# Convolution edges to VectorE, its tap and rest a step later; modulation group 5 into pass two; the second quarter's roots earlier

## The chip, the cores and the metric

The kernel runs on 1 core of a Trainium2 chip. The metric is the device time of one execution in microseconds (us), the median of several runs. One core has five engines with queues of their own: TensorE (PE: matrix products and transposes into PSUM), VectorE (DVE), ScalarE (ACT), GpSimd (POOL) and SyncE (SP, which here only issues transfers). Each engine works its queue strictly in the program's order; an instruction that waits holds up all that stand behind it on its engine. Transfers (DMA) are issued from the queues of SP and POOL and run beside the engines.

## The reference

One layer of a diffusion backbone over 2048 tokens of 1024 channels, with a short gated convolution as the mixer and an expert-choice mixture of 16 experts:

```
m = silu(c) @ ada_w + ada_b;  sh1, sc1, g1, sh2, sc2, g2 = split(m, 6)
h  = rms_norm(x, norm_g[0]) * (1 + sc1) + sh1
gate_b, gate_c, v = split(h @ w_in, 3)
x1 = x + g1 * ((gate_b * dwconv3(gate_c * v, conv_w)) @ w_out)
h2 = rms_norm(x1, norm_g[1]) * (1 + sc2) + sh2
aff = softmax(h2 @ router);  each expert takes its 256 best tokens
out = x1 + g2 * scatter_add(gate * (silu(xs @ wg) * (xs @ wu)) @ wd)
```

`dwconv3` is a depthwise convolution over 3 neighbouring tokens: y[t] = w0 u[t-1] + w1 u[t] + w2 u[t+1]. All is float32; each matrix product is made of three products of parts (high x high, low x high, high x low).

## The kernel before

The scheduling is by hand: on each engine the instructions stand in the order in which the Python code calls them.

*The input product* h @ w_in takes the 2048 tokens as four quarters of 512. First come two channel blocks of the first quarter and the second (`in_mm`, `in_out`), while the modulation's columns and the normalized rows come in. The loop over `g` in 0..3 does the first quarter; in its last round the second quarter's four blocks of 128 rows are prepared: a sum of squares (`rstd_of`, line 287 on ScalarE or 285 on VectorE), a root in two GpSimd operations (288, 290), and a scaling of the rows (`norm_x`, 415 or 417). `to_hl` then transposes them on TensorE (424).

*The two passes.* What is left of the product runs in 148 steps. A *unit* is two blocks of products for two halves; it has seven steps of 12 matmuls (lines 869 to 871), the seven products of a fast 2x2 block scheme, summed into three PSUM banks. Steps 0 to 63 are pass one (quarters one and two), where unit 8 has eight steps without the scheme (56 to 63); steps 64 to 147 are pass two (quarters three and four). Units come in threes: two make `gate_c` and `v` of a channel block, the third the `gate_b` of both. `unit_step` issues a step's products and copies a bank out on ScalarE (933) after steps 0, 1, 2, 4 and 6 of a unit; step 2 adds onto the bank of step 0, so its first product waits for the copy-out of step 0. VectorE adds a bank to the copied rows one step later (935). The blocks of weights are made three or four steps ahead: a high part on ScalarE (848), a low part on VectorE (849), and sums of blocks on VectorE (855 to 861).

*The order around the change.* `at(n, f)` puts a function into step n's list; the list runs before the step's own products. Behind the last step n of a unit of the first kind, `conv_start` is put at n + 1 (the product gate_c * v on VectorE, 881; the edge columns `v[:, 0:2]` from `carry` by a GpSimd copy, 882, in pass two a cleared last column, 884; the middle tap on ScalarE, 886) and `conv_rest` at n + 2 (the outer taps on VectorE, 890 and 892, and in pass one the edge kept in `carry`, 895). Behind a unit of the second kind `conv_gate` is put at n + 1 and n + 2 (900; a store to `vscr` from GpSimd's queue, 903 or 905, and a kept column, 906). The rows of a unit lie in five buffers, `wide`.

*Modulation groups 2 to 5* (g1, sh2, sc2, g2) are each a sum over eight blocks of 128 rows of `ada_w`. `ada_step(g, t)` adds block t - 1 on VectorE (562, 564), loads block t + 1 from GpSimd's queue (551) into one of four buffers `b4`, and at t = 9 ends the group: two products with a matrix of ones on TensorE (571) and two additions (572); groups 2 to 4 are then stored to `rows` (576). Group 5 stands at steps 36 to 47, groups 3, 2, 4 at steps 68 to 136, one t every 11/4 steps. The same buffers `b4` hold the rows `fu` that `load_full` and `refill` bring for pass two from step 47 to 67.

*Constants* for the later search are made by a generator, one piece at each of steps 4 to 43; `group_of` fills two tiles on GpSimd (120, 128) and compares them on VectorE (121 to 130).

Of the kernel before, what the change touches and what calls it, by code (L numbers as in the profile page):

```python
# [7 lines left out]
F32 = mybir.dt.float32  # L8
# [9 lines left out]
P = 128  # L18
# [28 lines left out]
def block_kernel(ctx: ExitStack, tc, x, c, ada_w, ada_b, norm_g, w_in, conv, w_out, router, wg, wu, wd, out):  # L47
# [63 lines left out]
    def constants(scratch):  # L111
        before = consts.tile([P, P], BF, name="before")
        nc.vector.tensor_scalar(before, jp, 0.0, None, op0=ALU.is_gt)
        ones_b = consts.tile([P, 1], BF, name="ones_b")
        nc.vector.memset(ones_b, 1.0)

        def group_of(name, shift, mask, pattern):

            row = consts.tile([P, 1], I32, name=name + "_i")
            nc.gpsimd.iota(row, pattern=[[0, 1]], base=0, channel_multiplier=1)  # L120
            nc.vector.tensor_scalar(row, row, shift, mask, op0=ALU.logical_shift_right, op1=ALU.bitwise_and)
            rowf = consts.tile([P, 1], F32, name=name + "_r")
            nc.vector.tensor_copy(rowf, row)
            n = 1
            for _, m in pattern:
                n *= m
            col = scratch("col", n)
            nc.gpsimd.iota(col, pattern=pattern, base=0, channel_multiplier=0, allow_small_or_imprecise_dtypes=True)
            t = consts.tile([P, n], F32R, name=name)
            nc.vector.tensor_scalar(t, col, rowf, None, op0=ALU.is_equal)  # L130
            return t, rowf

        yield
        same, _ = group_of("same", 3, E - 1, [[1, E], [0, 8]])
        yield
        sameq, _ = group_of("sameq", 3, NF - 1, [[0, P // (8 * NF)], [1, NF], [0, 8]])
        yield
        rep, repf = group_of("rep", 5, 3, [[1, 4]])
        block, _ = group_of("block", 5, 3, [[1, 4], [0, 32]])
        yield  # L140
        tri = consts.tile([P, P], BF, name="tri")
        nc.vector.tensor_mul(tri, block.bitcast(F32), before)
        mult = consts.tile([P, 5], F32, name="mult")
        nc.gpsimd.iota(mult, pattern=[[4, 5]], base=1, channel_multiplier=0, allow_small_or_imprecise_dtypes=True)
        nc.vector.tensor_scalar(mult, mult, repf, None, op0=ALU.add)
        stepq = consts.tile([P, N_FEW[0] + N_FEW[1], 3], F32, name="stepq")
        biasq = consts.tile([P, N_FEW[0] + N_FEW[1], 2], F32, name="biasq")
        for i in range(N_FEW[0] + N_FEW[1]):
            lo = i >= N_FEW[0]
            unit = 1.0 if lo else float(1 << LOW_FEW)  # L150
            if i % 3 == 0:
                yield
            st = unit * float(FEW) ** (N_FEW[0] + lo * N_FEW[1] - 1 - i)
            nc.gpsimd.tensor_scalar(stepq[:, i], mult[:, 0:3], st, None, op0=ALU.mult)
            nc.gpsimd.tensor_scalar(biasq[:, i], mult[:, 3:5], -st, 0.5 * unit, op0=ALU.mult, op1=ALU.add)
        yield
        needq = consts.tile([P, 5, 4], F32, name="needq")
        nc.gpsimd.memset(needq[:, 0:3], float(CAP))
        nc.gpsimd.memset(needq[:, 3:5], float(2 * CAP - L))
        slot_r = consts.tile([P, P], BF, name="slot_r")  # L160
        nc.gpsimd.iota(slot_r, pattern=[[1, P]], base=0, channel_multiplier=0,
                       allow_small_or_imprecise_dtypes=True)
        yield
        step = consts.tile([P, N_HI + N_LO], F32, name="step")
        bias = consts.tile([P, N_HI + N_LO, 2], F32, name="bias")
        for i in range(N_HI + N_LO):
            if i % 5 == 4:
                yield
            st = (1 << LOW) * 4.0 ** (N_HI - 1 - i) if i < N_HI else 4.0 ** (N_HI + N_LO - 1 - i)
            nc.gpsimd.memset(step[:, i:i + 1], st)  # L170
            for j in range(2):
                nc.gpsimd.memset(bias[:, i, j:j + 1], 0.5 * (float(1 << LOW) if i < N_HI else 1.0) - (j + 2) * st)
        need = consts.tile([P, 3], F32, name="need")
        nc.gpsimd.memset(need[:, 0:1], float(CAP))
        nc.gpsimd.memset(need[:, 1:3], float(2 * CAP - L))
        zero1 = consts.tile([P, 4], F32, name="zero1")
        nc.gpsimd.memset(zero1, 0.0)
        cnts = [consts.tile([P, 4], F32R, name=f"cnt{i}") for i in range(2)]
        zero1 = zero1[:, 0:1]
        aux = consts.tile([P, E, NB, 5], BF, name="aux")  # L180
        yield
        nc.gpsimd.iota(aux[:, :, :, 0], pattern=[[0, E], [0, NB]], base=0, channel_multiplier=1,
                       allow_small_or_imprecise_dtypes=True)
        yield
        nc.gpsimd.iota(aux[:, :, :, 1], pattern=[[0, E], [1, NB]], base=0, channel_multiplier=0,
                       allow_small_or_imprecise_dtypes=True)
        quick = sameq, rep, stepq, biasq, needq
        return before, ones_b, tri, slot_r, step, bias, need, zero1, cnts, aux, same, quick
# [180 lines left out]
    with tc.tile_pool(name="mix", bufs=1) as mix, ExitStack() as ctx_mixd:  # L369
# [63 lines left out]
        def low_x(q, k, full):  # L433
            nc.vector.tensor_sub(hl[q, k][:, 1], full, hl[q, k][:, 0].bitcast(F32))
# [213 lines left out]
        for g in range(4):  # L648
            k = 2 * g
            more_g = g < 3  # L650
            ada_fix(g, 0)
            full = scale_x(0, k)
            ada_fix(g, 1)
            if g:
                low_w(g, 1)
                low_w(g, 2)
            if more_g:
                ada_cols(g + 1, 0, 1)
            low_x(0, k, full)
            keep(k, full)  # L660
            mm_pair(0, k)
            turn_x(0, k + 1)
            full = scale_x(0, k + 1)
            if more_g:
                ada_cols(g + 1, 1, 5)
            low_x(0, k + 1, full)
            keep(k + 1, full)
            mm_pair(1, k)
            if more_g:
                turn_x(0, k + 2)  # L670
                high_w(g + 1)
                ada_cols(g + 1, 5, KD)
            else:
                rs = [rstd_of(xq[1][b], junk_tile()) for b in range(4)]
                for b in range(4):
                    norm_x(1, b, None, rs[b])
            mm_pair(0, k + 1)
            if g < 2:
                load_ada_cols(g + 2)
                load_w(g + 2)  # L680
            if g == 1:
                load_x(1)
            if more_g:
                ada_sum(g + 1)
                low_w(g + 1, 0)
            else:
                in_out(pair[0], 0, 0)
                to_hl(1, 0)
            mm_pair(1, k + 1)
# [188 lines left out]
        def conv_start(ps_, ct, c, v):  # L878

            o = v[:, 2:2 + 2 * QT]  # L880
            nc.vector.tensor_mul(o, c[:, 2:2 + 2 * QT], o)
            nc.gpsimd.tensor_copy(v[:, 0:2], carry[:, ct, 0:2])
            if ps_:
                nc.gpsimd.memset(v[:, 2 * QT + 2:2 * QT + 3], 0.0)
            n = 2 * QT + ps_
            nc.scalar.activation(c[:, 0:n], v[:, 1:1 + n], AF.Copy, scale=cw[1][:, ct:ct + 1])

        def conv_rest(ps_, ct, c, v):
# [3 lines left out]
            nc.vector.scalar_tensor_tensor(c[:, 0:n], v[:, 2:2 + n], cw[2][:, ct:ct + 1], c[:, 0:n],  # L892
                                           op0=ALU.mult, op1=ALU.add)
            if not ps_:
                nc.gpsimd.tensor_copy(carry[:, ct, 0:2], v[:, n:n + 2])

        def conv_gate(ps_, ct, gate):
            n = 2 * QT + ps_
# [2 lines left out]
            if ps_:  # L901
                nc.gpsimd.tensor_mul(c[:, 0:1], c[:, 0:1], carry[:, ct, 2:3])
                nc.gpsimd.dma_start(vscr[:, ct, L - n:L], c[:, 0:n])
            else:
                nc.gpsimd.dma_start(vscr[:, ct, 0:n - 1], c[:, 1:n])
                nc.gpsimd.tensor_copy(carry[:, ct, 2:3], gate[:, n + 1:n + 2])

        def behind_unit(u, n, x, y):
            (m, ct), (_, ct2) = units[u]
# [4 lines left out]
            else:  # L914
                convs[ct] = x
                at(n + 1, lambda: conv_start(ps_, ct, x, y))
                at(n + 2, lambda: conv_rest(ps_, ct, x, y))

        q0, q1 = slice(2, 2 + QT), slice(2 + QT, 2 + 2 * QT)

# [78 lines left out]
        for n in range(4):  # L999
# [9 lines left out]
            at(25 + 4 * n, lambda j=n: save_sums(j))  # L1009
            at(27 + 4 * n, lambda j=n: save_last(j))  # L1010
            at(47, lambda s=n: load_full(6 + s))
        for t in range(KD + 2):
            at(36 + t * 5 // 4, lambda t=t: ada_step(5, t))
        for s, n in enumerate((51, 52, 53, 54, 55, 56, 57, 58, 59, 60, 61, 62, 64, 65, 66, 67)):
            at(n, lambda s=s: refill(6 + s))
        for t in range(3 * KD + 2):
            for i, g in enumerate((3, 2, 4)):
                if 0 <= t - KD * i < KD + 2:
                    at(n1 + 4 + t * 11 // 4, lambda g=g, t=t - KD * i: ada_step(g, t))
        made = []  # L1020
        consts_of = constants(lambda name, n: hl_tile([P, n], F32, name))

# [749 lines left out]
```

## Time and profile before

| | us |
|---|---|
| median of 3 runs | 1869.77 (1867.82 to 1870.92) |
| the profiled execution | 1868.36 |
| its span, first to last instruction | 1866.3 |
| TensorE busy in it | 1798.3 |
| VectorE, ScalarE, GpSimd busy | 1276.3, 916.9, 333.1 |
| mean granted clock of TensorE | 0.986 |

In the profile's rows a line's instructions stand as `out<-in` with the tiles' names; a bracket such as `[2.16 <-ACT cx L933]` is the idle time of the engine just before, and what ended it. The granted clock (PEclk) is 1.00 at full speed and 0.50 at half. The first pass runs from about 105 to 302 us, the second to 543 us; then come the output product and router to about 750 us, the search, and the experts to the end.

### The profile page before, as it was taken

The page shows a single profiled execution, that of the slowest core. Times are in us where ns is not written, and L with a number is a line of the kernel's source. Part 1 is how long each engine was busy: PE and PEld are TensorE (multiplying, and loading weights), DVE is VectorE, ACT ScalarE, POOL GpSimd, SP SyncE. Part 2 cuts the span into 40 slices and gives each one's busy share as a digit, 9 for nine tenths or more (in the row PEclk, how much of TensorE's full clock was granted, in tenths as well). Part 3 has the DMA queues.
Part 4 walks back from the last instruction along what each step waited for, and adds up shares of the span by engine and source line. Part 5 has one row for each costly group of instructions (what it writes and reads, how often), then busy time and mean ns, then how long its engine had stood idle before and what let it go on. Part 6 is the DMA issues. An engine that isn't in the chain of part 4 may idle for free.

```text
span 1866.3 us, 29372 instructions
## 1 busy us (share of the span) xinstructions
PE 1798.3 (96%) x11415; PEld 1595.0 (85%) x11415; DVE 1276.3 (68%) x1804; ACT 916.9 (49%) x1246; POOL 333.1 (18%) x500
## 2 busy tenths in 40 slices
PE   7999989999999999599999999999999999999997
PEld 6778868878788887498899999999999999999996
DVE  6687777867776677787665765666666576666653
ACT  4555445333345555475454554455455454545541
POOL 2325210101112223100102210210211121021002
PEclk9999999999999999799999999999999999999999
DMA  9656656434467897476878788787878878788774
GB/s 340 206 187 206 224 192 221 150 114 147 136 227 236 246 261 225 149 225 204 223 222 260 222 242 244 250 233 227 262 213 244 259 225 237 233 258 235 224 228 80
DMA packets 309771, 406.78 MB, mean 218 GB/s; under 512 B 103284, under 2 KB 174240, under 8 KB 309632
## 3 DMA queue, kind: packets, MB, share of 16 engines
q1 hardware_dynamic: 283632, 312.59, 55.0%
q0 software_dynamic: 26000, 92.33, 16.7%
q8 instruction: 89, 1.46, 0.3%
q14 instruction: 50, 0.41, 0.1%
HBM read 318.34 MB, written 63.98 MB: 205 GB/s over the span
## 4 chain that ended last, share of the span: by engine, by line
PE 82%; DVE 6%; DMA 4%; issue 4%; ACT 3%; POOL 1%; POOLq 0%; SPq 0%; ACTq 0%; DVEq 0%
PE pm L1595 12%; PE pm L1597 12%; PE pm L1599 12%; PE pm L1664 6%; PE pm L1662 6%; PE pm L1663 6%; PE pm L869 5%; PE pm L870 5%; PE pm L871 5%; PE pm L1124 2%; PE pm L1125 2%; PE pm L1127 2%; DMA hl<-hl 1%; PE pm L511 1%; PE pm L512 1%
## 5 line engine op out<-in xcount | busy, mean ns | idle before, releaser
L248 DVE TENSOR_TENSOR ws<-raw,ws 128x1024 fp32r<-128x1024 f32 x390 | 463.5, 1221 | 273.9 <-ACT ws L238 273.5
L238 ACT ACTIVATE ws<-raw 128x1024 fp32r<-128x1024 f32 x390 | 394.3, 1052 | 410.0 <-PE pm L1599 325.6
L1595 PE MATMUL pm<-xT,ws 128*128 128x256 f32 x2048 | 568.6, 278 | 1.3 <-ACT xT L1574 1.3
L1597 PE MATMUL pm<-xT,ws 128*128 128x256 f32 x2048 | 567.3, 277 | 1.9 <-DVE xT L1575 1.8
L1599 PE MATMUL pm<-xT,ws 128*128 128x256 f32 x2048 | 566.8, 277 | 0.0
L1597 PEld LDWEIGHTS pm<-xT,ws 128*128 128x128 f32 x2048 | 386.0, 188 | 3.9 <-DVE xT L1575 2.1
L1595 PEld LDWEIGHTS pm<-xT,ws 128*128 128x128 f32 x2048 | 385.9, 188 | 3.0 <-ACT xT L1574 1.8
L1599 PEld LDWEIGHTS pm<-xT,ws 128*128 128x128 f32 x2048 | 385.9, 188 | 0.0
L1692 POOL DMA_INDIRECT out_dram<-ot,idx x30 | 104.9, 3498 | 588.8 <-DVE ot L1681 584.8
L1664 PE MATMUL pm<-ws,hT 128*128 128x512 f32 x504 | 198.3, 394 | 0.0
L1662 PE MATMUL pm<-ws,hT 128*128 128x512 f32 x504 | 198.1, 393 | 0.0
L1663 PE MATMUL pm<-ws,hT 128*128 128x512 f32 x504 | 197.0, 391 | 0.0
L869 PE MATMUL pm<-tg,sb 128*128 128x512 f32 x472 | 187.2, 397 | 8.2 <-ACT cx L933 8.1
L871 PE MATMUL pm<-tg,sb 128*128 128x512 f32 x472 | 184.6, 391 | 0.0
L870 PE MATMUL pm<-tg,sb 128*128 128x512 f32 x472 | 184.5, 391 | 0.0
L849 DVE TENSOR_TENSOR sb<-raw,sb 128x512 fp32r<-128x512 f32 x144 | 98.5, 688 | 85.8 <-ACT sb L848 85.4
L869 PEld LDWEIGHTS pm<-tg,sb 128*128 128x128 f32 x472 | 89.0, 189 | 31.5 <-ACT cx L933 13.0
L848 ACT ACTIVATE sb<-raw 128x512 fp32r<-128x512 f32 x144 | 88.6, 626 | 53.8 <-DVE raw L855 23.5
L1664 PEld LDWEIGHTS pm<-ws,hT 128*128 128x128 f32 x504 | 94.7, 188 | 20.0
L1663 PEld LDWEIGHTS pm<-ws,hT 128*128 128x128 f32 x504 | 94.6, 188 | 19.8
L1662 PEld LDWEIGHTS pm<-ws,hT 128*128 128x128 f32 x504 | 94.7, 188 | 18.6
L871 PEld LDWEIGHTS pm<-tg,sb 128*128 128x128 f32 x472 | 89.0, 189 | 18.9
(385 smaller groups left out, 2626.4 us busy)
## 6 DMA issues: line engine op xcount, KB each, us to landing
raw<-in_moe_w_down_dram SPq DMA_DIRECT2D x128, 512.0 KB, 4.7
raw<-in_moe_w_gate_dram SPq DMA_DIRECT2D x126, 512.0 KB, 5.1
raw<-in_moe_w_up_dram SPq DMA_DIRECT2D x126, 512.0 KB, 4.1
raw<-in_sc_w_in_dram SPq DMA_DIRECT2D x42, 512.0 KB, 4.4
xt<-in_x_dram SPq DMA_DIRECT2D x32, 512.0 KB, 7.2
aw<-in_ada_w_dram POOLq DMA_DIRECT2D x32, 512.0 KB, 4.1
fu<-fscr SPq DMA_DIRECT2D x23, 512.0 KB, 4.5
hl<-in_ada_w_dram SPq DMA_DIRECT2D x32, 256.0 KB, 6.3
```

The costliest lines, as they stand in the source:

```text
L238: nc.scalar.activation(t[:, 0], raws[n_high], AF.Copy)
L248: (eng or nc.vector).tensor_sub(t[:, 1, ..., s], raw[..., s], t[:, 0, ..., s].bitcast(F32))
L869: nc.tensor.matmul(o, t[:, 0, j], r[:, 0], start=(first and j == 0), stop=False, skip_group_check=True)
L870: nc.tensor.matmul(o, t[:, 1, j], r[:, 0], start=False, stop=False, skip_group_check=True)
L871: nc.tensor.matmul(o, t[:, 0, j], r[:, 1], start=False, stop=end, skip_group_check=True)
L1595: nc.tensor.matmul(o, w[:, 0, j, c0], xT[:, 0, k], start=(k == 0 and f % 2 == 0), stop=False, skip_group_check=True)
L1597: nc.tensor.matmul(o, w[:, 0, j, c0], xT[:, 1, k], start=False, stop=False, skip_group_check=True)
L1599: nc.tensor.matmul(o, w[:, 1, j, c0], xT[:, 0, k], start=False, stop=(k == KD - 1), skip_group_check=True)
L1662: nc.tensor.matmul(ps[s], h, w[:, 0, j], start=(k == 0), stop=False)
L1663: nc.tensor.matmul(ps[s], h, w[:, 1, j], start=False, stop=False)
L1664: nc.tensor.matmul(ps[s], l, w[:, 0, j], start=False, stop=(k == KD - 1))
L1692: st = nc.gpsimd.indirect_dma_start(out=out_rows, out_offset=bass.IndirectOffsetOnAxis(ap=idx_of[e][:, s:s + 1], axis=0), in_=ots[s], in_o ...
```

## The change

Four edits. (1) `group_of` is a generator now: GpSimd's fills come in one step, VectorE's comparisons in the next; two more pauses lie around `block` and `mult`. (2) In the last round of the first quarter the four `rstd_of` of the second quarter move up: blocks 0 and 2 (squares on ScalarE) behind the second `ada_fix`, blocks 1 and 3 (squares on VectorE) behind `low_x`; of the scalings, blocks 0 and 2 go to ScalarE. (3) The convolution's edge copies, cleared columns and kept columns go from GpSimd to VectorE, the edge ahead of the product; the middle tap becomes `conv_tap`, at n + 2, and `conv_rest` goes to n + 3. (4) Group 5 leaves steps 36 to 47 and goes ahead of groups 3, 2, 4 in pass two; the t of all four lie at listed steps 67 to 137: steps 1, 3, 5 of a unit, and 1, 2, 3, 5 of every third unit.

```diff
@@ group_of
             row = consts.tile([P, 1], I32, name=name + "_i")
             nc.gpsimd.iota(row, pattern=[[0, 1]], base=0, channel_multiplier=1)
-            nc.vector.tensor_scalar(row, row, shift, mask, op0=ALU.logical_shift_right, op1=ALU.bitwise_and)
-            rowf = consts.tile([P, 1], F32, name=name + "_r")
-            nc.vector.tensor_copy(rowf, row)
...
             nc.gpsimd.iota(col, pattern=pattern, base=0, channel_multiplier=0, allow_small_or_imprecise_dtypes=True)
+            yield
+            nc.vector.tensor_scalar(row, row, shift, mask, op0=ALU.logical_shift_right, op1=ALU.bitwise_and)
+            rowf = consts.tile([P, 1], F32, name=name + "_r")
+            nc.vector.tensor_copy(rowf, row)
@@ the loop over g
             ada_fix(g, 1)
+            if not more_g:
+                rs = {b: rstd_of(xq[1][b], junk_tile()) for b in (0, 2)}
...
             low_x(0, k, full)
+            if not more_g:
+                rs.update({b: rstd_of(xq[1][b], junk_tile(), nc.vector) for b in (1, 3)})
...
-                rs = [rstd_of(xq[1][b], junk_tile()) for b in range(4)]
                 for b in range(4):
-                    norm_x(1, b, None, rs[b])
+                    norm_x(1, b, None if b % 2 else nc.scalar, rs[b])
@@ conv_start
             o = v[:, 2:2 + 2 * QT]
+            nc.vector.tensor_copy(v[:, 0:2], carry[:, ct, 0:2])
+            if ps_:
+                nc.vector.memset(v[:, 2 * QT + 2:2 * QT + 3], 0.0)
             nc.vector.tensor_mul(o, c[:, 2:2 + 2 * QT], o)
-            nc.gpsimd.tensor_copy(v[:, 0:2], carry[:, ct, 0:2])
-            if ps_:
-                nc.gpsimd.memset(v[:, 2 * QT + 2:2 * QT + 3], 0.0)
+
+        def conv_tap(ps_, ct, c, v):
             n = 2 * QT + ps_
             nc.scalar.activation(c[:, 0:n], v[:, 1:1 + n], AF.Copy, scale=cw[1][:, ct:ct + 1])
@@ conv_rest
-                nc.gpsimd.tensor_copy(carry[:, ct, 0:2], v[:, n:n + 2])
+                nc.vector.tensor_copy(carry[:, ct, 0:2], v[:, n:n + 2])
@@ conv_gate
-                nc.gpsimd.tensor_copy(carry[:, ct, 2:3], gate[:, n + 1:n + 2])
+                nc.vector.tensor_copy(carry[:, ct, 2:3], gate[:, n + 1:n + 2])
@@ behind_unit
                 at(n + 1, lambda: conv_start(ps_, ct, x, y))
-                at(n + 2, lambda: conv_rest(ps_, ct, x, y))
+                at(n + 2, lambda: conv_tap(ps_, ct, x, y))
+                at(n + 3, lambda: conv_rest(ps_, ct, x, y))
@@ the lists of steps
-        for t in range(KD + 2):
-            at(36 + t * 5 // 4, lambda t=t: ada_step(5, t))
...
-        for t in range(3 * KD + 2):
-            for i, g in enumerate((3, 2, 4)):
+        ada_at = [n1 + N_GROUP * v + i for v in range(N_GROUP + 4) for i in ((1, 2, 3, 5) if v and v % 3 == 0 else (1, 3, 5))]
+        ada_at = [n for n in ada_at if n > n1 + 2]
+        for t in range(4 * KD + 2):
+            for i, g in enumerate((5, 3, 2, 4)):
                 if 0 <= t - KD * i < KD + 2:
-                    at(n1 + 4 + t * 11 // 4, lambda g=g, t=t - KD * i: ada_step(g, t))
+                    at(ada_at[t], lambda g=g, t=t - KD * i: ada_step(g, t))
```

More of the change, by code (lines that the diff above doesn't have):

```diff
@@ L133, in constants @@
         yield
-        same, _ = group_of("same", 3, E - 1, [[1, E], [0, 8]])
+        same, _ = yield from group_of("same", 3, E - 1, [[1, E], [0, 8]])
         yield
-        sameq, _ = group_of("sameq", 3, NF - 1, [[0, P // (8 * NF)], [1, NF], [0, 8]])
+        sameq, _ = yield from group_of("sameq", 3, NF - 1, [[0, P // (8 * NF)], [1, NF], [0, 8]])
         yield
-        rep, repf = group_of("rep", 5, 3, [[1, 4]])
-        block, _ = group_of("block", 5, 3, [[1, 4], [0, 32]])
+        rep, repf = yield from group_of("rep", 5, 3, [[1, 4]])
+        yield
+        block, _ = yield from group_of("block", 5, 3, [[1, 4], [0, 32]])
         yield
@@ L144, in constants @@
         nc.gpsimd.iota(mult, pattern=[[4, 5]], base=1, channel_multiplier=0, allow_small_or_imprecise_dtypes=True)
+        yield
         nc.vector.tensor_scalar(mult, mult, repf, None, op0=ALU.add)
```

## The prediction

> **What bounds the kernel now.** I read the page first, then the waits of TensorE, then its busy time in stretches of 20 us, then the timeline around each gap.
>
> ```profile
> PE 1798.3 (96%) x11415; PEld 1595.0 (85%) x11415; DVE 1276.3 (68%) x1804; ACT 916.9 (49%) x1246; POOL 333.1 (18%) x500
> ```
>
> TensorE (PE) is busy 96% of the 1866.3 us span, so only its gaps, and time at a lower clock, can be won. The change touches the program up to the end of pass two, about 540 us. There these stretches are not full (start:end, length, PE busy, then the other engines; PEclk is the granted clock):
>
> ```profile
> 60.00:80.00 20.00, 16.35 (x76) 12.79 (x75) 12.49 (x20) 13.24 (x22) 8.36 (x17) 0.91 0.28 103
> 120.00:140.00 20.00, 17.84 (x79) 14.47 (x78) 14.73 (x31) 10.74 (x20) 8.07 (x20) 1.00 0.34 121
> 200.00:220.00 20.00, 18.98 (x92) 15.53 (x92) 16.14 (x24) 8.97 (x15) 5.71 (x13) 1.00 0.71 239
> 240.00:260.00 20.00, 14.58 (x48) 9.87 (x47) 14.70 (x22) 4.70 (x9) 4.91 (x6) 0.83 0.76 242
> 380.00:400.00 20.00, 17.72 (x69) 13.80 (x68) 12.58 (x17) 6.50 (x12) 1.85 (x5) 0.91 0.44 132
> 460.00:480.00 20.00, 18.78 (x83) 15.19 (x82) 14.37 (x19) 7.49 (x13) 1.45 (x4) 1.00 0.44 127
> ```
>
> Idle PE is 20 minus the first figure: 3.65, 2.16, 1.02, 5.42, 2.28 and 1.22 us. Three stretches also lose clock: 0.91 over 20 us costs 20 x 0.09 = about 1.7 us, 0.83 costs 3.4 us. Who is waited for, in the waits view (total, times, longest; the first row is of the stretch 0 to 80 us):
>
> ```profile
> PE pt L424 <- DVE xt L417: 3.6, 4, 1.1
> PE pm L869 <- ACT cx L933: 8.1, 5, 2.3
> PE pt L571 <- DVE acc L564: 4.0, 1, 4.0
> ```
>
> So three causes: transposes that wait for the second quarter's normalized rows (3.6), block products that wait until ScalarE (ACT) has copied a PSUM bank out (8.1 in five gaps), and the end of modulation group 5 (4.0).
>
> **The change, part by part.** *Convolution.* Why ScalarE is late is seen in the rows around three of the gaps:
>
> ```profile
> 129.03 1.22 DVE L881 TENSOR_TENSOR cy<-cx,cy 128x1024 f32<-128x1024 f32 x1
> 130.36 1.15 ACT L886 ACTIVATE cx<-cy,v_col 128x1024 f32<-128x1024 f32 x1 [3.67 <-DVE cy L881]
> 132.04 0.50 PE L869 MATMUL pm<-tg,sb 128*128 128x512 f32 x1 [2.16 <-ACT cx L933]
> ...
> 242.05 0.60 ACT L933 ACTIVATE cy<-pm 128x512 f32<-128x512 f32 x1 [2.95 <-POOL carry L906]
> ...
> 386.11 0.56 POOL L551 DMA_DIRECT2D aw<-in_ada_w_dram  x1 [2.47 <-DMA rows<-dst]
> 386.67 0.20 POOL L882 COPY cy<-carry 128x2 f32<-128x2 f32 x1
> 386.90 1.15 ACT L886 ACTIVATE cx<-cy,v_col 128x1025 f32<-128x1025 f32 x1 [6.60 <-POOL cy L884]
> ```
>
> The tap L886 stands in ScalarE's queue ahead of the copy L933 of the unit's first product. At 130 us it waits for VectorE (DVE), whose product L881 stands behind constants; at 387 us for a tiny GpSimd (POOL) copy behind a load that itself waits for `rows<-dst`. At 242 us the copy-out itself waits for GpSimd's edge copy L906 to free a buffer. The program's order on ScalarE at the first convolution, before:
>
> ```order
> L848 ACTIVATE sb<-raw 128x512
> L287 ACTIVATE junk,ss<-xt 128x1024
> L886 ACTIVATE cx<-cy,v_col 128x1024
> L933 ACTIVATE cx<-pm 128x512
> L848 ACTIVATE sb<-raw 128x512
> L287 ACTIVATE junk,ss<-xt 128x1024
> L933 ACTIVATE cy<-pm 128x512
> ```
>
> and now (L894 is the tap, L942 the copy-out, L290 the square):
>
> ```order
> L854 ACTIVATE sb<-raw 128x512
> L290 ACTIVATE junk,ss<-xt 128x1024
> L942 ACTIVATE cx<-pm 128x512
> L854 ACTIVATE sb<-raw 128x512
> L290 ACTIVATE junk,ss<-xt 128x1024
> L894 ACTIVATE cx<-cy,v_col 128x1024
> L942 ACTIVATE cy<-pm 128x512
> ```
>
> The tap moved behind the copy of `cx`, which the step after next needs, and now stands ahead of `cy`, which is needed four steps later. On VectorE, at the same place, the product L881 stood before behind two constants (`rep`, `block`) whose first operations wait for GpSimd:
>
> ```order
> L935 TENSOR_TENSOR cx<-cx,pm 128x512
> L849 TENSOR_TENSOR sb<-raw,sb 128x512
> L859 TENSOR_TENSOR raw<-raw 128x512
> L121 TENSOR_SCALAR rep_i<-rep_i 128x1
> L123 CAST rep_r<-rep_i 128x1
> L130 TENSOR_SCALAR rep<-col,rep_r 128x4
> L121 TENSOR_SCALAR block_i<-block_i 128x1
> L123 CAST block_r<-block_i 128x1
> L130 TENSOR_SCALAR block<-col,block_r 128x128
> L881 TENSOR_TENSOR cy<-cx,cy 128x1024
> ```
>
> and now (L890 is the product):
>
> ```order
> L944 TENSOR_TENSOR cx<-cx,pm 128x512
> L855 TENSOR_TENSOR sb<-raw,sb 128x512
> L865 TENSOR_TENSOR raw<-raw 128x512
> L887 COPY cy<-carry 128x2
> L890 TENSOR_TENSOR cy<-cx,cy 128x1024
> L855 TENSOR_TENSOR sb<-raw,sb 128x512
> L867 TENSOR_TENSOR raw<-raw 128x512
> L420 TENSOR_SCALAR xt<-xt,rstd 128x1024
> ```
>
> The constants moved to later steps, and L887, the edge copy taken from GpSimd, stands before the product. Its price:
>
> ```profile
> L882 POOL COPY cy<-carry x14: 178/198/730, 128.1 to 517.3; 128x2 f32<-128x2 f32 x14
> L906 POOL COPY carry<-cy x3: 200/948/2807, 177.7 to 312.7; 128x1 f32<-128x1 f32 x3
> L542 DVE COPY carry<-pm x2: 149/150/150, 98.8 to 111.7; 128x1 f32<-128x1 f32 x2
> ```
>
> 14 + 6 + 6 copies x 0.15 us, and 8 clears of at most that, is 5 us of VectorE spread over 435 us, under products on TensorE; without that cover it is 5 us. The gain is the five gaps: 8.1 us, and the clock at 380 (1.7) with its 2.28 us gap: 9.8. What is late next is the rest (two passes over 1024 columns), a step later; its readers, the gates, come at least a unit (seven steps) later, so I take 0. Bounds: half of the five gaps stay (+4.9), or nothing more.
>
> *Modulation group 5.* In pass one its picks are one step apart:
>
> ```profile
> 249.35 1.29 DVE L564 SCALAR_TENSOR_TENSOR acc<-aw,s_col,acc 128x1024 f32<-128x1024 f32 x1 [1.44 <-DMA aw<-in_ada_w_dram]
> 250.78 3.75 PE L571 MATMUL pt<-acc,ones_f 128*128 128x512 f32 x4 [4.03 <-DVE acc L564]
> ...
> L564 DVE SCALAR_TENSOR_TENSOR acc<-aw,s_col,acc x28: 1276/1279/1286, 226.3 to 505.4; 128x1024 f32<-128x1024 f32 x28
> DMA to landing us min/median/max: 3.9/4.1/7.3
> ```
>
> The last of its eight loads lands late, VectorE waits, TensorE waits 4.03 us and then runs at half clock: 4.03 + 3.4 = 7.4 us leave pass one. Its matmuls L571 only change place. A rule stands against the clock term: the Trainium skill, "TensorE: Matmul & The Clock Gate" (section "What's actually happening"), has the clock halved after an idle window of about 3.4 us. By it the 2.28 us gap at 380 and the 1.14 us pieces at 60 would lose no clock, and the sum would be 3.4 us smaller; the rows have 0.91 in both stretches, so the rows decide.
>
> In pass two eight loads on GpSimd's queue, eight adds of 1.28 and two additions join: 11.6 us of VectorE over some 200. Picks now lie at steps 1, 3, 5 of a unit, and at 2 as well after a gate unit; the gates' stores to `vscr` share GpSimd's queue with the loads. Three of the four ends come two or three steps after the last add. Group 5's comes one step after it. VectorE's order at its end before, in pass one (L564 the last add, L572 the additions behind the matmuls):
>
> ```order
> L564 SCALAR_TENSOR_TENSOR acc<-aw,s_col,acc 128x1024
> L935 TENSOR_TENSOR cx<-cx,pm 128x512
> L849 TENSOR_TENSOR sb<-raw,sb 128x512
> L857 TENSOR_TENSOR raw<-raw 128x512
> L572 TENSOR_TENSOR g2b<-pt,g2b 128x512 x2
> ```
>
> and now, in pass two:
>
> ```order
> L908 TENSOR_TENSOR cx<-cx 128x1024
> L855 TENSOR_TENSOR sb<-raw,sb 128x512
> L567 SCALAR_TENSOR_TENSOR acc<-aw,s_col,acc 128x1024
> L908 TENSOR_TENSOR cx<-cx,cy 128x1024
> L855 TENSOR_TENSOR sb<-raw,sb 128x512
> L575 TENSOR_TENSOR g2b<-pt,g2b 128x512 x2
> L565 TENSOR_SCALAR acc<-aw,s_col 128x1024
> ```
>
> The last add L567 and the additions L575 moved between the gates L908 of a gate unit. The rows of that place before, and the product step after it:
>
> ```profile
> 364.03 0.69 DVE L849 TENSOR_TENSOR sb<-raw,sb 128x512 fp32r<-128x512 f32 x1 [0.30 <-ACT sb L848]
> 365.34 0.39 PE L869 MATMUL pm<-tg,sb 128*128 128x512 f32 x1
> ```
>
> The add would start when L849 ends, at 364.72, and end at 366.0, against a step that starts at 365.34: TensorE waits about 0.7 us. Bounds: 0, or 2 us if VectorE is a whole operation later.
>
> *Second quarter.* Rows of the end of the first quarter:
>
> ```profile
> 56.99 0.78 ACT L429 ACTIVATE hl<-pt,sh,A 128x512 fp32r<-128x512 f32 x1 [2.31 <-PE pt L424]
> 58.33 1.05 ACT L287 ACTIVATE junk<-xt 128x1024 bf16<-128x1024 f32 x1
> 58.47 0.69 DVE L434 TENSOR_TENSOR hl<-full,hl 128x512 fp32r<-128x512 f32 x1 [3.45 <-ACT full L430]
> 60.60 0.63 POOL L288 TENSOR_SCALAR ss<-ss 128x1 f32<-128x1 f32 x1 [0.20 <-ACT junk L287]
> 61.31 0.55 POOL L290 TENSOR_TENSOR rstd<-ss,mhalf 128x1 f32<-128x1 f32 x1
> 65.50 0.68 DVE L524 TENSOR_TENSOR u<-cs,pm 128x512 f32<-128x512 f32 x1
> 65.64 0.48 PE L424 MATMUL pt<-identf,xt 128*128 128x128 f32 x1 [1.14 <-DVE xt L417]
> 69.20 0.15 DVE L542 COPY carry<-pm 128x1 f32<-128x1 f32 x1
> ...
> L285 DVE SCALAR_TENSOR_TENSOR junk<-xt x2: 1225/1226/1226, 6.7 to 9.5; 128x1024 bf16<-128x1024 f32 x2
> L415 ACT ACTIVATE xt<-xt,rstd x2: 1132/1132/1132, 9.2 to 10.2; 128x1024 f32<-128x1024 f32 x2
> ...
> 41.71 1.07 SPq L408 DMA_DIRECT2D xt<-in_x_dram  x2
> DMA to landing us min/median/max: 9.3/9.3/9.3
> ```
>
> Four squares, four GpSimd roots and four scalings run in a row at 58 to 65.6 us. Now two squares (2.1 us) fall into ScalarE's idle 2.31 us before 56.99, and two on VectorE (2.5) into its idle 3.45 before 58.47. The last rows of x were asked for by 42.8 and took 9.3 us, so they are there at 52.1. The roots start near 56; at 0.75 to 1.3 us each they end by 59 to 61. Scalings, two of 1.13 on ScalarE from 58.4 and two of 0.75 on VectorE, end near 60.6, and the transposes can start at 61.0, where TensorE comes free. Gone: 3.65 idle and 1.7 clock. What is late next: the first quarter's channel work, from `u` to the last read of its PSUM bank, takes 3.85 us (65.50 to 69.35) and starts behind a 0.58 us copy, 4.4 in all; TensorE has some 3.4 us of work before it wants that bank. So about 1.0 comes back: net 4.35, between 2.5 and 5.3.
>
> The roots' two small GpSimd operations now run beside VectorE's squares. The Trainium skill, "GPSIMD Engine Reference" (section "1. Specifications"), says its SBUF interface is shared with VectorE, with contention against instructions of two SBUF inputs; by it each of them could wait out a square of 1.2 us, and another 1 us would be lost here.
>
> **Sum.** -9.8 (convolution) -7.4 (group 5) -4.35 (second quarter) +0.7 = -20.85. The profiled execution took 1868.36: 1847.5. The median shown is 1.4 above that execution: **1849 us**.
>
> **Rivals.** *VectorE becomes the bound in pass two.* These stretches show its load there, and one of pass one:
>
> ```profile
> 300.00:500.00 200.00, 196.40 (x846) 159.17 (x845) 152.75 (x201) 77.67 (x133) 25.70 (x57) 0.99 0.48 149
> 220.00:240.00 20.00, 20.00 (x90) 16.57 (x89) 18.31 (x25) 6.10 (x11) 5.08 (x10) 1.00 0.82 283
> ```
>
> The added 11.6 us raise 76% to about 82%, and products, rests and adds now share the units' early steps. Against it: at 220 to 240 us TensorE had no gap with VectorE at 92%. If each of eight added adds costs TensorE its 1.28, 10 us come back: 1859.
>
> *The tap still blocks.* If ScalarE finds the product unready a step later too, or the buffers still wait for GpSimd's stores, the five gaps stay: -20.85 + 9.8 = -11: 1860. Against it: a whole step was given, 12 of the 90 products that fill 20 us, 2.7 us, and the longest gap is 2.28.
>
> *The late load moves along* (slower). What happened at 250 us, a last add waiting for its load and the clock lost behind it, costs 7.4. If GpSimd, held by its wait for `rows<-dst`, issues loads so late that all four ends in pass two pay it, 4 x 7.4 = 29.6 against 20.85: +8.8: 1878. It decides only if a load is issued less than its landing time before its add; a load goes out two picks ahead, 5.4 us at the closest, against 4.1 in the median, so it takes landings of 7.3 throughout. (A group's first load has one pick alone, one step in the closest case, but behind it stand the two additions L575.)
>
> *Nothing to be seen*: the gains are taken back at the next stage's loads. The stages behind start from TensorE's own chain, so little speaks for it: 1869.
>
> **How the numbers follow.** My forecast 0.76, VectorE 0.08, tap 0.07, late load 0.04, nothing 0.05. A difference under 0.2% (3.7 us) cannot be told from none: faster 0.91, same 0.05, slower 0.04. The range: all terms at their best (-9.8 -7.4 -5.3, and the clock of one more stretch, -1.7) gives 1845, and I add 3 for what the idle rows leave out at each restart: 1842. At the other side the first two rivals give 1860; so 1842 to 1860.
>
> **What would show it.** Right: no PE wait of over 0.5 us for the copy-out (now L942) in either pass; PEclk 1.00 in all stretches from 60 to 540 us; transposes of the second quarter without a wait; a wait of about 0.7 at group 5's end in pass two. Wrong: L942 still in the waits of PE with several us, a wait of the adds L567 for `aw`, or VectorE's splits (now L855) named as PE's releaser in pass two.

## The result, and the profile after

| | before | after |
|---|---|---|
| median of 4 runs, us | 1869.95 | 1846.03 (1843.38 to 1848.51) |
| ratio | | 0.9873, 95% interval 0.9853 to 0.9894 |
| the profiled execution, us | 1868.36 | 1848.51 |
| its span, us | 1866.3 | 1846.7 |

The forecast was 1849 us, within 1842 to 1860. Its sum, -20.85, was made for the profiled execution, and stands against -19.85 there. Three of its terms came out within 0.3 us in this pair of executions; one was too small by 3.15, and a new loss that it did not name took 1.4 of that back. One of ten executions of the kernel that makes the constants' edit alone took 6741 us at a mean granted clock of 0.395; no ratio here contains it.

The page of the changed kernel, busy time by engine, in the form of the line that the prediction shows of before:

```profile
PE 1791.2 (97%) x11415; PEld 1594.1 (86%) x11415; DVE 1281.7 (69%) x1840; ACT 919.6 (50%) x1244; POOL 320.2 (17%) x466
```

Its stretches of 20 us (start:end, length, busy PE, PEld, DVE, ACT, POOL, then PEclk):

```profile
60.00:80.00 20.00, 19.07 (x99) 15.45 (x98) 14.11 (x23) 14.34 (x21) 8.97 (x18) 1.00 0.40 143
160.00:180.00 20.00, 18.07 (x85) 14.85 (x84) 17.02 (x25) 10.25 (x18) 9.37 (x61) 1.00 0.55 173
240.00:260.00 20.00, 20.00 (x90) 16.54 (x89) 16.24 (x26) 12.34 (x20) 0.00 (x0) 1.00 0.49 165
340.00:360.00 20.00, 19.50 (x83) 15.18 (x82) 14.82 (x21) 6.75 (x12) 4.39 (x7) 1.00 0.71 233
380.00:400.00 20.00, 20.00 (x86) 15.85 (x85) 17.06 (x25) 7.90 (x13) 2.14 (x4) 1.00 0.45 132
520.00:540.00 20.00, 19.75 (x92) 16.35 (x92) 13.54 (x16) 8.09 (x11) 2.31 (x3) 0.91 0.82 270
```

TensorE is full and at full clock where the copy-outs and group 5 had stopped it (240, 380). What is left of idle time from 60 to 560 us is in three waits (waits view of TensorE; total, times, longest):

```profile
PE pt L427 <- DVE xt L420: 2.8, 2, 1.9
PE pt L574 <- DVE acc L567: 0.5, 1, 0.5
PE pl L1315 <- ACT st L1312: 0.2, 1, 0.2
```

The copy-out L942 is in no wait. The second row is the wait forecast at group 5's end. The first is 0.8 us at the second quarter and 1.9 us near 172 us, which was 0.36 before: the new loss.

**A finer measure.** The 148 steps of the two passes do the same 12 products each, so the time from a step's first product (line 869 before, 875 now) to the next step's can be set side by side, step by step; a plain step takes 2.72 us. From step 0 to step 147 before took 435.07 us, after 417.05. The 18.02 us, and the 4.28 us by which step 0 starts earlier, fall as follows:

| steps | what stood there | gain by step lengths, us | forecast |
|---|---|---|---|
| 8-9, 36-37, 45, 93-95, 121-122 | the five copy-out gaps, with clock | 11.08 | 9.8 |
| 50-51, 68, 72-73, 79-80, 100-101, 142-143 | short waits for copy-outs | 1.87 | 0 |
| 46-47, 86-87 | group 5 leaves, its end comes in | 8.95 - 2.50 = 6.45 | 6.7 |
| 15, 23 | roots and normalizations of quarters three and four | -1.40 | 0 |
| before step 0 | second quarter: first block product to step 0, 83.16 to 78.61 | 4.55 | 4.35 |

In step 121 the end of another group now stands, 0.45 us, which is taken out. The sum is 22.55; the first block product itself came 0.27 later, so step 147 starts 22.3 us earlier. Not every row is known to a tenth: the way to step 0 took 82.70 to 83.86 us in the six kernels with the old roots, and 77.64 to 78.74 in seven with the new ones, 5.0 apart in the mean; steps 46 and 47 were 7.9 to 9.8 us too long in the six kernels that keep group 5 there. From there to the end no instruction has changed its place, and still it takes 1328.70 us in place of 1325.95: 2.75 come back. Where, is told with the clock below.

### The profile page after: what moved, and what is told of

Its sections match the earlier page's. It is cut to its first block, busy times and chain, and to the rows that moved or that the text cites. A ratio compares the mean times of both kernels' runs of the same rounds, so it can differ in the third digit from the quotient of the medians.

```text
span 1846.7 us, 29333 instructions
## 1 busy us (share of the span) xinstructions
PE 1791.2 (97%) x11415; PEld 1594.1 (86%) x11415; DVE 1281.7 (69%) x1840; ACT 919.6 (50%) x1244; POOL 320.2 (17%) x466
## 4 chain that ended last, share of the span: by engine, by line
PE 88%; DVE 5%; DMA 2%; ACT 2%; issue 1%; POOL 0%; SPq 0%; POOLq 0%; DVEq 0%; ACTq 0%
PE pm L1604 12%; PE pm L1606 12%; PE pm L1608 12%; PE pm L876 7%; PE pm L877 7%; PE pm L875 7%; PE pm L1673 6%; PE pm L1671 6%; PE pm L1672 6%; PE pm L1133 2%; PE pm L1134 2%; PE pm L1136 2%; PE pm L514 1%; PE pm L515 1%; PE pm L517 1%
```

## The experiments

Each kernel was timed beside the kernel before. "Steps" is the time from step 0 to step 147; it tells a few tenths of a us apart, the times do not.

| run | ratio to before, 95% interval | steps, us |
|---|---|---|
| before | | 435.07 |
| after; the same again | 0.9873 (0.9853-0.9894); 0.9873 (0.9857-0.9890) | 417.05; 417.03 |
| convolution's edit alone | 0.9947 (0.9930-0.9963) | 423.51 |
| tap and rest later alone | 0.9926 (0.9910-0.9943) | 424.25 |
| edge copies alone | 0.9984 (0.9974-0.9994) | 431.86 |
| constants alone | 1.0010 (1.0000-1.0020) | 439.01 |
| group 5 alone | 0.9952 (0.9935-0.9970) | 426.32 |
| roots alone | 0.9962 (0.9946-0.9978) | 435.97 |
| after, tables later | 0.9866 (0.9848-0.9884) | 415.41 |
| after, tables written three times | 0.9873 (0.9854-0.9893) | 416.35 |
| after, constants back | 0.9863 (0.9847-0.9880) | 415.38 |
| after, both mends | 0.9858 (0.9841-0.9874) | 414.65 |
| the same, other order of roots | 0.9853 (0.9836-0.9869) | 414.67 |

**The convolution's edit, whole and in parts.** Four kernels make the edit on the kernel before: whole; only the delay; only the copies; only the constants.

```diff
@@ delay
-                at(n + 2, lambda: conv_rest(ps_, ct, x, y))
+                at(n + 2, lambda: conv_tap(ps_, ct, x, y))
+                at(n + 3, lambda: conv_rest(ps_, ct, x, y))
@@ copies (and so the clears and the two copies into carry)
-            nc.gpsimd.tensor_copy(v[:, 0:2], carry[:, ct, 0:2])
+            nc.vector.tensor_copy(v[:, 0:2], carry[:, ct, 0:2])
@@ constants
-        same, _ = group_of("same", 3, E - 1, [[1, E], [0, 8]])
+        same, _ = yield from group_of("same", 3, E - 1, [[1, E], [0, 8]])
```

> Before, with the convolution's edit alone (edge copies on VectorE, tap and rest a step later, constants spread). From the first block product of step 0 to that of step 147 the steps took 435.07 us before. Forecast's theory (ScalarE's late copy-outs cost five gaps of 8.1 us and 1.7 us of clock): 9.8 us shorter, 425.3. Second theory (TensorE's idle rows hide the short waits: the weight loader's rows show 13.0 us in 12 waits for the same copy-out): 12.7 us shorter, 422.4, less 1.6 if the two index tables L185 and L188 also come to stand beside a normalization L420 as they did in the changed kernel, so 424.0. Rival (the tap still blocks): 435.

> Before, with tap and rest a step later alone; the edge copies stay on GpSimd and the constants where they were. If the place of the tap in ScalarE's queue is the cause of the gaps, all go but the one at 243.7 us, where the copy-out itself waits for GpSimd's edge copy: the steps 10.8 us shorter (12.7 less 1.9). If the slow GpSimd copies are the cause, the gaps at 243.7 and 388.6 stay: 6 to 7 us shorter at most. If nothing but both together helps: under 3 us.

> Before, with the edge copies and clears on VectorE alone, tap and rest not moved. If the tap's place in the queue is the cause: only the gaps at 243.7 and 388.6 go, about 1.9 and 4.2 us, so 6 us shorter; the short waits of 0.3 us at every unit of pass two and the gap of 2.2 us at 132 stay. If the GpSimd copies were all of it: 10 to 12.7 us shorter. If VectorE pays for the 34 small instructions on the path: 5 us longer at most.

> Before, with the constants' steps spread alone. Theory of the forecast: only the gap at 132 us goes, 2.4 us with its restart. If the index tables then fall beside a normalization of the fourth quarter, as in the changed kernel, one such normalization takes 2.4 in place of 0.75 us and TensorE waits up to 1.6 us more near 175 us: 0.8 shorter in all. Rival (the constants do nothing to TensorE): 0.

The whole edit took 11.57 us out of the steps: the second theory, not the forecast's 9.8. Why TensorE's rows showed too little is seen in the weight loader's waits in the kernel before, 100 to 545 us, and in the rows of one short wait:

```profile
PEld pm L869 <- ACT cx L933: 13.0, 12, 2.7
...
528.63 0.58 ACT L933 ACTIVATE cx<-pm 128x512 f32<-128x512 f32 x1
529.26 0.19 PEld L869 LDWEIGHTS pm<-tg,sb 128*128 128x128 f32 x1 [0.45 <-ACT cx L933]
```

The loader had 12 waits for the copy-out, where TensorE's own rows had five with 8.1 us. In a short one the loader stands for 0.45 us while the last matmul is still drawn as busy; the step is 0.19 us late, the next 0.17, and no idle time appears. This happened at five of the eight convolutions of pass two; two of the others are among the five gaps.

Of the three parts the delay alone does almost all of it, 10.83 of 11.57 (the 11.57 are what is left after a loss of 1.56 at step 23, told below), and closes the gap at 132 us as well. The rows of that place with the delay alone, ScalarE's and VectorE's (L936 is the copy-out, L888 the tap, L881 the product):

```profile
127.28 0.60 ACT L936 ACTIVATE cx<-pm 128x512 f32<-128x512 f32 x1 [0.52 <-PE pm L871]
...
129.10 1.22 DVE L881 TENSOR_TENSOR cy<-cx,cy 128x1024 f32<-128x1024 f32 x1
...
130.41 1.15 ACT L888 ACTIVATE cx<-cy,v_col 128x1024 f32<-128x1024 f32 x1 [0.98 <-POOL ss L288]
```

The product is as late as before (129.03), and so is the tap, but the copy-out has gone ahead of both. The rest (the outer taps) moved along with the tap; it can't have held this copy-out, since it stood a step behind it already before. The prediction had blamed three things, and of these the tap's place in ScalarE's queue is the cause of most of the gaps. The copies alone gave 3.21, less than the 6 that the tap's theory expected of them: the gap at 388 went but for 0.3 us, and that at 243 us was only shortened by 0.45 us. Yet they are not idle: with the delay alone step 67 grew by 1.72 us. ScalarE's and GpSimd's rows of that kernel (L936 is its copy-out, L908 its edge copy):

```profile
304.47 2.15 POOL L908 COPY carry<-cx 128x1 f32<-128x1 f32 x1
...
306.65 0.60 ACT L936 ACTIVATE cy<-pm 128x512 f32<-128x512 f32 x1 [3.59 <-POOL carry L908]
```

A copy of one column takes 2.15 us on GpSimd here (0.20 at its shortest in the same kernel) and holds the buffer that the copy-out fills. On VectorE it takes 0.15, and the whole edit has no wait at that step.

The constants alone made the steps 3.94 us longer, where 0.8 less was expected. Of the gap at 132 us they took 1.24, and at 180 us they lost 5.5 (rows of VectorE, GpSimd and TensorE, and the two windows of 3.41 us around):

```profile
171.96 0.75 DVE L420 TENSOR_SCALAR xt<-xt,rstd 128x1024 f32<-128x1024 f32 x1
177.48 2.17 DVE L420 TENSOR_SCALAR xt<-xt,rstd 128x1024 f32<-128x1024 f32 x1
...
177.80 1.88 POOL L909 COPY carry<-cy 128x1 f32<-128x1 f32 x1
...
179.70 1.33 PE L427 MATMUL pt<-identf,xt 128*128 128x128 f32 x5 [3.34 <-DVE xt L420]
...
174.92:178.34 3.42, 1.45 (x8) 0.96 (x7) 3.42 (x5) 2.12 (x4) 1.45 (x9) 1.00 0.89 255
178.34:181.76 3.42, 2.06 (x8) 1.87 (x9) 1.90 (x2) 1.47 (x3) 2.87 (x3) 0.50 1.02 357
```

The normalization took 2.17 us in place of 0.75. Beside it stands GpSimd's edge copy, which this kernel has kept; the index tables that the expectation blamed start behind it, at 179.64. Which of the two held the other, the rows don't show.

**The normalization of 2.4 us.** The same instruction is what TensorE waits for in the changed kernel, where none of these edge copies is left on GpSimd. Its rows there, VectorE and GpSimd:

```profile
167.37 0.75 DVE L420 TENSOR_SCALAR xt<-xt,rstd 128x1024 f32<-128x1024 f32 x1
169.83 2.41 DVE L420 TENSOR_SCALAR xt<-xt,rstd 128x1024 f32<-128x1024 f32 x1
...
170.11 0.87 POOL L185 IOTA aux<- 128x256 bf16 x1
170.72 0.97 POOL L188 IOTA aux<- 128x256 bf16 x1
```

The longer row of constants pushed the last two, index tables on GpSimd, from 158 and 163 us to 170 us, beside the last normalization. Three kernels ask whether the tables are the cause: tables three steps later, tables written three times, and the constants at their old steps.

```diff
         aux = consts.tile([P, E, NB, 5], BF, name="aux")
-        yield
+        yield; yield; yield; yield
```

> The changed kernel, with the two index tables L185 and L188 three steps later on GpSimd, behind the fourth quarter's normalizations; the other engines' orders are unchanged. Theory (a GpSimd index table and a VectorE normalization in SBUF hold each other up): the normalization at 169.8 us takes 0.75 in place of 2.41 us, TensorE's wait of 1.93 us there falls to under 0.4, and steps 0 to 147 take 1.55 us less than the 417.05 of the changed kernel: 415.5. Rival (VectorE was only late, from the edge copy and the gates): the wait stays at 1.9.

> The changed kernel, with each of the two index tables L185 and L188 written three times in a row. Theory (the two engines hold each other up): the normalization beside them takes some 3.5 us more than 2.41, if it waits them out, and TensorE's wait of 1.93 grows by as much; at least by 1. Rival (no tie between them): the normalization stays at 2.41 and the wait at 1.93, since nothing reads the tables in this stage.

> The changed kernel without the first of its edits: the constants at their old steps again. If the tap's later place alone closed the gap at 132 us, the spread is worth nothing there and costs 1.65 near 170 us: steps 0 to 147 take 415.4 in place of 417.05. If the spread is what closed that gap: 2.45 come back and 1.65 go, 417.9.

With the tables later, and nothing else moved on any engine, the last normalization takes 0.76 us and step 23 is 1.65 us shorter:

```profile
167.12 0.75 DVE L420 TENSOR_SCALAR xt<-xt,rstd 128x1024 f32<-128x1024 f32 x1
169.58 0.76 DVE L420 TENSOR_SCALAR xt<-xt,rstd 128x1024 f32<-128x1024 f32 x1
```

So the tables cause it there. With the tables thrice the expectation missed its size and its sign:

```profile
169.43 1.70 DVE L420 TENSOR_SCALAR xt<-xt,rstd 128x1024 f32<-128x1024 f32 x1
...
169.71 0.87 POOL L185 IOTA aux<- 128x256 bf16 x1
170.65 2.18 POOL L186 IOTA aux<- 128x256 bf16 x2
```

The normalization took 1.70, not 2.41 or more: it ended 0.55 after the first table, and the next two tables took 2.18. It waits out a table, then, but not all that are queued; by what rule the turn changes between the engines is open. The Trainium skill, "SBUF — State Buffer" (section "Who interferes with whom"), says that a VectorE scaling from SBUF to SBUF in its two-port mode and a GpSimd instruction take a pair of ports in turn, each for the whole instruction. Rows of 0.75, 1.70 and 2.41 us for one and the same operation agree with that in so far as one waits for the other; which came first they don't settle, since the normalization is drawn 0.28 us ahead of the first table in both kernels and still waited.

Without the constants' edit the steps take 415.38, 1.67 less than the changed kernel's, and the gap at 132 us stays closed. That edit is worth nothing beside the delay, and costs 1.67 us.

**Group 5 alone, roots alone.**

```diff
@@ group 5
-        for t in range(KD + 2):
-            at(36 + t * 5 // 4, lambda t=t: ada_step(5, t))
...
-            for i, g in enumerate((3, 2, 4)):
+            for i, g in enumerate((5, 3, 2, 4)):
@@ roots
+                rs = {b: rstd_of(xq[1][b], junk_tile()) for b in (0, 2)}
...
-                rs = [rstd_of(xq[1][b], junk_tile()) for b in range(4)]
```

> Before, with modulation group 5 in pass two and the new picks alone. Forecast's theory: 7.4 us leave pass one (4.0 of wait and 3.4 of clock at 250 us), 0.7 come back at the group's end in pass two: 6.7 shorter. Rival (VectorE the bound in pass two): 10 us come back, 3.3 longer. Rival (late loads at all four ends): 8.8 to 22 longer. The convolution's gaps may move with the picks: the wait for the copy-out at 388.6, which stood behind a GpSimd load, may go (then 4.2 more) or turn up at other units.

> Before, with the second quarter's roots moved up alone. Forecast's theory: 4.35 us shorter at the start of step 0, of it 1.7 clock; the changed kernel's trace has 4.28. The rest of the program unchanged, so the last stages start 4.3 earlier too. Rival (the gain is taken back by the loads of the first steps): 0 to 1.

Group 5 alone gave 8.75 us of steps in place of 6.7. Its own part was as in the whole change, 8.95 less 2.56. The rest is the convolution's: the gap at 243 us went too (1.55; why was not followed), and that at 388 us (3.9 with its clock), where the GpSimd load that had stood ahead of the edge copy is no longer picked; a new copy-out wait of 1.55 came at step 72, and 1.6 of clock were lost behind the gap at 132. The gain at 388 is had from either edit, and most of that at 243, which is one reason why the parts alone add up to more than the whole: the table's split between the convolution and group 5 is not the only one possible. The roots alone shortened the way from the first block product to step 0 from 83.16 to 78.53 us; against the expectation the steps did not stay as they were but took 0.90 us longer, 0.81 of it at step 23, where TensorE waited 1.2 us for the last normalization. Why that came later is not shown.

**Mending what is left.** Two kernels: the tables later and group 5's end one step later still (its picks at steps 86, 88 and 89 in place of 86, 87 and 88); then also block 1 of the second quarter squared ahead of a low part on VectorE.

```diff
-        ada_at = [n for n in ada_at if n > n1 + 2]
+        ada_at = [n + (n1 + 22 < n < n1 + 25) for n in ada_at if n > n1 + 2]
@@ the order of roots
-            if not more_g:
-                rs = {b: rstd_of(xq[1][b], junk_tile()) for b in (0, 2)}
             if g:
                 low_w(g, 1)
                 low_w(g, 2)
+            if not more_g:
+                rs = {b: rstd_of(xq[1][b], junk_tile(), nc.vector if b == 1 else None) for b in (1, 0, 2)}
...
-                rs.update({b: rstd_of(xq[1][b], junk_tile(), nc.vector) for b in (1, 3)})
+                rs[3] = rstd_of(xq[1][3], junk_tile(), nc.vector)
```

> The changed kernel, with the two index tables three steps later and with group 5's end two steps behind its last add in place of one (the ends' other picks unchanged). Theory: the tables' 1.65 us as measured alone, and the wait of 0.74 us at the group's end goes: steps 0 to 147 take 414.65 in place of 417.05. Rival for the end (VectorE is behind all through the gate unit, so the add is late a step later too): 415.4. The time, against the kernel before: 2.4 below the changed kernel's, so about 1843.6.

> As the version with both mends, and the second quarter's block 1 squared ahead of the low part L437 on VectorE, in an idle stretch of 1.4 us, so that its root stands first on GpSimd and only one root meets a VectorE square. Theory (the four roots in a row, one of them stretched from 0.55 to 1.44 beside a square, keep the last scaling late): the wait of 0.8 us of the transposes at 61 us goes and step 0 starts 0.8 earlier than the 100.72 of the version without it. Rival (what follows the roots, the first quarter's copies on ScalarE, ends last anyway): under 0.2.

> The changed kernel itself again, beside the other three: 1846 us, and the same step times (417.05 from step 0 to step 147) within 0.2, since nothing in these steps hangs on anything but the order; what differs from its first profile is only where TensorE's clock is halved.

Both mends gave 2.40 us of steps, as expected: the end of group 5 now costs 1.77 us, what the ends of the other groups cost, in place of 2.50. For the roots, the rows of GpSimd and VectorE in the changed kernel, and then GpSimd's in the last one:

```profile
56.35 1.22 DVE L288 SCALAR_TENSOR_TENSOR junk<-xt 128x1024 bf16<-128x1024 f32 x1
56.56 1.44 POOL L293 TENSOR_TENSOR rstd<-ss,mhalf 128x1 f32<-128x1 f32 x1
61.05 0.55 POOL L293 TENSOR_TENSOR rstd<-ss,mhalf 128x1 f32<-128x1 f32 x1
61.63 0.75 DVE L420 TENSOR_SCALAR xt<-xt,rstd 128x1024 f32<-128x1024 f32 x1 [0.72 <-POOL rstd L293]
```

```profile
54.90 1.03 POOL L293 TENSOR_TENSOR rstd<-ss,mhalf 128x1 f32<-128x1 f32 x1
56.77 0.55 POOL L293 TENSOR_TENSOR rstd<-ss,mhalf 128x1 f32<-128x1 f32 x1
58.59 0.55 POOL L293 TENSOR_TENSOR rstd<-ss,mhalf 128x1 f32<-128x1 f32 x1
...
60.00:80.00 20.00, 19.62 (x102) 16.12 (x101) 14.07 (x24) 15.03 (x23) 6.94 (x14) 1.00 0.42 153
```

The roots end at 59.1 in place of 61.6, the wait of 0.8 for the scaling is gone, and TensorE is busy 19.62 of 20 us in place of 19.07: 0.55, not the 0.8 expected, because a wait of 0.4 for a copy of ScalarE (line 449) comes next. The start of step 0 itself (100.43) cannot show it; it moved by 1.7 us between runs of kernels that are the same up to there (99.25 to 100.96). This version ran at 1841.29 us (1839.80 to 1843.26), the changed kernel beside it at 1845.07 (1843.65 to 1846.62). No run of the one reaches the other; the intervals of their ratios to before overlap.

## Why the prediction was right, and where it was not

The causes of the three gains were named rightly, and the experiments bear them out. That the sum met the profiled execution within 1.0 us is luck in part: step 147 started 22.3 us earlier, 1.45 more than the sum, and 2.75 came back behind it, 1.7 of them with the clock. The medians differ by 23.9. Two of its figures are not what its own terms give: the rival of the tap that still blocks comes to 1858.8 (1849 and 9.8), not 1860, and all terms at their best to 1845.6, not 1845.

**The tap and the copy-outs.** The place was right: the delay alone shows it. The size failed at the step "the gain is the five gaps: 8.1 us, and the clock": 9.8 forecast, 12.95 by the steps. 1.87 of the difference are the waits too short to leave an idle row, 1.28 the restarts (0.07 to 0.17 behind four of the five gaps) and the rest of their length. The 3 us that the range allowed for restarts nearly cover both, and no row stood behind that figure. 1.55 and 3.9 of the 12.95, at 243 and 388 us, came with group 5's move alone as well. The constants were a wrong part of the reason: the gap at 132 us closes without them.

**The constants at no cost.** The prediction followed VectorE's constants and said only that they moved to later steps. It did not follow the rest of the generator, which runs on GpSimd: all that stands behind the new pauses comes later, the two tables among it. A loss of 1.65 us was the price.

**Group 5.** 7.4 out and 0.7 back were forecast, 7.18 (8.95 less the 1.77 that an end costs anywhere) and 0.73 measured; so close a match of the first is luck, since the 8.95 lay between 7.9 and 9.8 us in the kernels that keep the group there. The end's rows:

```profile
346.25 1.28 DVE L567 SCALAR_TENSOR_TENSOR acc<-aw,s_col,acc 128x1024 f32<-128x1024 f32 x1
...
347.68 1.96 PE L574 MATMUL pt<-acc,ones_f 128*128 128x512 f32 x4 [0.50 <-DVE acc L567]
```

Moving the end one step on removed it, as its reason (an add one step ahead of its reader) says.

**Second quarter.** 4.35 forecast, 4.55 measured (5.0 between the means), with a wrong reason for what comes back. The prediction put 1.0 us on the PSUM bank of the first quarter. No row waits for that bank; the last scaling was late, by 0.8, since the four roots took until 61.6, 0.6 past the 59 to 61 given for them. The rule weighed there fits: by the GPSIMD Engine Reference of the Trainium skill (section "1. Specifications") a root could wait out a square, and one did, 1.44 in place of 0.55 us.

**The rivals.** VectorE did not become the bound. Its load in pass two rose to 82%, as forecast (200 us, the stretch that answers to 300 to 500 before):

```profile
278.00:478.00 200.00, 199.50 (x870) 162.80 (x869) 165.00 (x227) 81.65 (x138) 25.95 (x48) 1.00 0.57 176
```

and every step of pass two took 2.72 us but those with a group's end. The late load did not decide, though a sign named for it is there; in VectorE's waits from 278 to 520 us stand

```profile
DVE acc L565 <- DMA aw<-in_ada_w_dram: 4.7, 2, 2.6
...
DVE acc L567 <- DMA aw<-in_ada_w_dram: 1.6, 3, 0.7
```

five late loads. None of them stood ahead of a group's end by so little that TensorE saw it. The tap still blocking, and nothing to be seen, are refuted by the steps.

**The clock.** Counted by the rows, it was right: the stretches at 60, 240 and 380 us have 1.00. The rule of the Trainium skill that the prediction set against it ("TensorE: Matmul & The Clock Gate", section "What's actually happening": half clock after an idle window) would have left 3.4 us out and does not hold here: the window from 386.22 us, shown below, was busy for 1.13 of its 3.41 us, and half clock followed. But the clock's terms are those of one execution: the stretch at half clock in the second quarter lasted 3.41 us in four of the six kernels with the old roots, and 6.83 in two. "PEclk 1.00 from 60 to 540" failed at one place, 530 us, which the change did not touch.

## What to carry to other kernels

Measure a gap by the distance of equal pieces of work on the bound engine, or by its loader's waits, not by its idle rows alone: short waits and restarts leave no idle time, and here made a quarter of the convolution's gain. When a generator or a list of chores gets a pause, follow every engine's chores behind the pause to where they land, and see what runs beside them. A copy or a tap that others wait behind on its engine belongs behind the copy that the bound engine needs next; this one move alone gave 10.8 us, and the convolution's whole edit 11.6.

## What the runs showed of the hardware

**The clock goes by windows of 3.41 us that don't follow the kernel.** All stretches at half clock, in 14 profiled executions, begin on one grid of 3.41 us within a run and last a multiple of it (but for the last, at the program's end); the grid lies elsewhere in the next. Busy PE and PEclk in windows of that grid: around the gaps at 132 and 388 us of the kernel before, around the same gap at 132 in the kernel with group 5 alone, and near 530 us in the changed kernel:

```profile
130.22:133.64 3.42, 1.59 (x7) 1.34 (x8) 1.12 (x3) 3.28 (x6) 0.00 (x0) 1.00 0.00 0
...
386.22:389.63 3.41, 1.13 (x6) 0.87 (x6) 0.55 (x1) 2.73 (x5) 0.68 (x3) 1.00 0.54 180
389.63:393.05 3.42, 3.42 (x10) 2.68 (x9) 3.23 (x4) 0.42 (x1) 0.00 (x0) 0.50 0.04 18
```

```profile
129.98:133.39 3.41, 1.51 (x7) 1.25 (x8) 1.11 (x3) 3.20 (x6) 0.00 (x0) 1.00 0.00 0
133.39:136.81 3.42, 3.42 (x10) 2.68 (x9) 3.03 (x6) 2.71 (x6) 2.65 (x6) 0.50 0.53 153
```

```profile
526.52:529.93 3.41, 3.16 (x26) 2.84 (x25) 3.41 (x4) 2.03 (x3) 1.92 (x3) 1.00 0.98 326
529.93:533.35 3.42, 3.42 (x10) 2.64 (x9) 1.84 (x3) 0.00 (x0) 0.39 (x1) 0.50 0.68 271
```

The first gap cost no clock in one run and 1.7 us in another, by where the windows cut it: 1.59 busy us in the window kept the clock, 1.51 lost it. The busy share alone does not settle it: among windows that were between 0.47 and 0.57 busy both came. Behind a window at full clock with over 0.62 of it busy by matmuls of 256 or 512 columns the clock was never lost. At 530 us it was lost after a window with hardly any idle time, but with small products in it (eight transposes and 16 products of 16 columns); this came in 5 of the 14 executions. The Trainium skill, "TensorE: Matmul & The Clock Gate" (section "What's actually happening"), says that the window of 3413 ns runs free of the kernel, and the trace agrees.

**That grid goes with most of the noise of this kernel.** Step 147 to the end has the same instructions in the same places in all 14 executions and took 1322.4 to 1328.7 us. Those with 8 windows at half clock in it (ahead of the last 10 us, where all have some) took 1322.4 and 1324.4, with 9 1324.2 and 1325.1, with 10 1325.9 to 1326.5, with 11 1327.0 to 1328.7; one with 12 took 1327.0. The kernel before was profiled with 10, the changed one with 11: one window is 1.7 of the 2.75 us that came back behind step 147, and where the other 1.05 went is open. The two lower of the changed kernel's first four runs, 1843.4 and 1843.8, have a mean clock of 0.990 and 0.991, the two upper, 1848.3 and 1848.5, 0.987 and 0.988.
